# The expert stage of a two-layer diffusion transformer: steps of four bundles in another order, tiled products, and the scatter in fp32r

## The chip, the cores and the metric

One core of a Trainium2 chip runs the whole program: TensorE (PE; its weight loads are shown as PEld), VectorE (DVE), ScalarE (ACT), GpSimd (POOL) and SyncE (SP), which issues most DMAs. The metric is the device time of one execution in microseconds (us).

## What is computed

Two layers on 256 tokens of 1024 features (and 256 context tokens). Layer 0 has a mixer and a dense feed-forward part; layer 1 has a mixer and then a mixture of experts, which the change is about:

```python
def moe_swiglu(t, wr, br, w1, w3, w2):
    tf = t.reshape(-1, shape[-1])
    logits = (tf @ wr + br).astype(jnp.float32)
    top_v, top_i = lax.top_k(logits, TOP_K)              # TOP_K = 2 of N_EXPERTS = 8
    gates = jax.nn.softmax(top_v, axis=-1)
    dense_gate = jnp.sum(jax.nn.one_hot(top_i, N_EXPERTS) * gates[..., None], axis=1)
    for e in range(N_EXPERTS):                           # w1, w3: 1024 x 2816, w2: 2816 x 1024
        out = out + dense_gate[:, e:e + 1] * swiglu(tf, w1[e], w3[e], w2[e])
```

All is fp32. The result is multiplied by a gate vector of the layer (G2 in the kernel) and added to the residual X.

## The kernel before

**Routing and dispatch.** route() finds each token's two experts, orders experts 1 to 7 by how many tokens they got, and gives each token a slot in its expert. The experts' numbers become registers on SP (values_load, L1359), since SP needs them for the addresses of the weights; expert 0 of the order is always expert 0 and needs none. dispatch() makes, for a "quad" of four groups of 32 slots, a 0/1 matrix P, gathers the tokens by products with P (L1400), transposes them (L1411) into X, and makes P's transpose PT and the gates gs of the slots (L1420 to L1431).

**Bundles.** BUNDLES has four: bundle 0 is expert 0 with one group of 32 ("alone"); bundle 1 has two quads on experts 1 and 2 (the first quad is all expert 1, called quad A here; the second, quad B, has experts 1, 2, 2, 2); bundle 2 has one quad on experts 5 and 6; bundle 3 two quads on experts 3, 4 and 7.

**Steps.** The 2816 hidden features are cut into chunks of 1024, 1024 and 768 (CHUNKS). A step t is one chunk of one bundle: up(t, 0) multiplies by w1 and applies silu, up(t, 1) multiplies by w3 and multiplies both, turn(t) transposes the result (L1547), down(t) multiplies by w2 and adds into the accumulators yacc (L1585, L1587). moe_phases gives the order: up(t, 0), down(t - 1), up(t, 1), then the next t. Before the change steps 0 to 2 are bundle 0, 3 to 5 bundle 1, and so on. Each up and down runs in quarters of 256 rows of weights. After a bundle's last chunk, finish() multiplies yacc by gs and G2 (L1603) and scatters it with fp32 products by PT (L1608), each added to X (L1610). Dispatch, turn and finish are generators: pump(), called after each quad and row block of an up or down, advances them, so that their products stand between the experts' own.

**Products.** In the alone bundle four 256-column products go to four 32-column tiles of the array (L1493, L1574). For the other quads products() issues one 128 x 128 product of up to 512 columns if all four groups have one expert (L1498: quad A), else four products in 32-column tiles (L1502). A product of fp32 operands is two records in the trace.

**Weights.** plan_moe lists every weight load (1 MiB, or 0.75 MiB for up in the last chunk) in the order of use. ahead() issues loads on SP (L200) for as many entries as the ring has tiles: nine (three of the weights pool and EXTRA = 6), and, from the expert stage on, the four tiles that held split weights in earlier stages (whi and wlo), 13 in all. A tile is free again when the products that read it are done. moe() extends the ring by the four after route(). A pool's tag with bufs=n has n buffers, and a new tile waits for the one it replaces.

Of the kernel before, what the change touches and what calls it, by code (L numbers as in the profile page):

```python
# [48 lines left out]
CHUNKS = ((0, 1024), (1024, 1024), (2048, 768))  # L49

# [61 lines left out]
class Net:  # L112
    def __init__(self, tc, I, out):
        self.tc, self.nc, self.I, self.out = tc, tc.nc, I, out
        self.es = ExitStack()
        self.cnt = {}
        self.xw = None
        self.ring = deque()
        self.share = self.after = None
        self.tasks = []  # L120
        self.plan, self.pos = [], 0
# [63 lines left out]
    def plan_w(self, key, src, shape, split=True):  # L185
        parts = src if isinstance(src, list) else [(0, 128, src)]
        self.plan.append(dict(key=key, parts=parts, shape=shape, split=split, raw=None, hl=None))

    def ahead(self, raws=None, splits=None):
# [1125 lines left out]
    def route(self, p, t, first):  # L1315
# [29 lines left out]
        R = t.tile([128, 7, 7], F32, name="R")  # L1345
# [32 lines left out]
    def dispatch(self, p, quad, X, out):  # L1378
# [29 lines left out]
        for m in range(2):  # L1408
# [3 lines left out]
            dst = X[:, m * 4:m * 4 + 4].rearrange("p k t -> p (k t)")  # L1412
            if m:
                v.tensor_copy(dst, pg)
            else:
                nc.scalar.activation(dst, pg, AF.Copy)
# [6 lines left out]
        PT = p.tile([128, 2, 128], F32, tag="PT1h", name="PT1h", bufs=4)  # L1423
        gs = p.tile([128, 1], F32, tag="gs", name="gs", bufs=4)
# [18 lines left out]
    def moe_phases(bundles):  # L1443

        n = len(bundles) * len(CHUNKS)
# [8 lines left out]
    def plan_moe(self, tag, bundles):  # L1454
        for kind, t, m in self.moe_phases(bundles):
            bundle = bundles[t // len(CHUNKS)]
            c0, n = CHUNKS[t % len(CHUNKS)]
            rs = sorted({r for quad in bundle for r, _ in quad})
            for i in range(4 if kind == "up" else n // 256):
                for r in rs:  # L1460
                    if kind == "up":
                        src = self.moe_src(("moe_w1", "moe_w3")[m], r, slice(i * 256, (i + 1) * 256), slice(c0, c0 + n))
                        self.plan_w((tag, kind, t, m, i, r), src, (2, n), False)
                    else:
                        src = self.moe_src("moe_w2", r, slice(c0 + i * 256, c0 + (i + 1) * 256), slice(0, D))
                        self.plan_w((tag, kind, t, m, i, r), src, (2, D), False)

    def experts(self, p, tag, bundles, started=None):
# [6 lines left out]
        nch = len(CHUNKS)  # L1475
        ready = {0: started} if started is not None else {}
        acc, st = {}, {}

        def start(b):
            if b in ready or b >= len(bundles):  # L1480
                return
# [6 lines left out]
        def products(quad, outs, lhs, w, n, first, last):  # L1488

            if quad[0] == quad[1]:  # L1490
                for s in range(n // 256):
                    ss = slice(s * 32, s * 32 + 32)
                    mm(outs[0][ss, 0:256], lhs[:, ss], w[quad[0][0]][:, s * 256:(s + 1) * 256], start=first, stop=last, tile_position=(0, s * 32))  # L1493
                return
            for h in range(len(outs)):
                cs = slice(h * 512, min(n, h * 512 + 512))
# [3 lines left out]
                for s, (r, _) in enumerate(quad):  # L1500
                    ss = slice(s * 32, s * 32 + 32)
                    mm(outs[h][ss, 0:cs.stop - cs.start], lhs[:, ss], w[r][:, cs], start=first, stop=last, tile_position=(0, s * 32))  # L1502

        def parts(quad, n):
            return [256] if quad[0] == quad[1] else [min(512, n - c) for c in range(0, n, 512)]

        def places(quad, n):
            return n // 8 if quad[0] == quad[1] else 128

        def experts_of(bundle):  # L1510
            return sorted({r for quad in bundle for r, _ in quad})

        def up(t, m):
            b, (c0, n) = t // nch, CHUNKS[t % nch]
            bundle = bundles[b]
            ph = [[self.ps("ph") for _ in parts(quad, n)] for quad in bundle]
            for i in range(4):
                w = {r: self.W((tag, "up", t, m, i, r)) for r in experts_of(bundle)}
                for k in range(2):
                    kk = i * 2 + k  # L1520
                    for q, quad in enumerate(bundle):
                        products(quad, ph[q], ready[b][q][0][:, kk], {r: x[:, k] for r, x in w.items()}, n, kk == 0, kk == 7)
                        self.pump()
# [3 lines left out]
            for q, quad in enumerate(bundle):  # L1527
                for h, wd in enumerate(parts(quad, n)):
                    ps = slice(0, places(quad, n))
# [6 lines left out]
        def turn(t):  # L1536

            b, (c0, n) = t // nch, CHUNKS[t % nch]
            hid = []
            for q, quad in enumerate(bundles[b]):  # L1540
                g = p.tile([128, 8, 128], F32, tag="gt", name="gt", bufs=2)
                m = places(quad, n)
                for h, wd in enumerate(parts(quad, n)):
                    pt = self.ps("ptg")
                    nf = wd // 128
                    for f in range(nf):
                        nc.tensor.transpose(pt[:, f * m:(f + 1) * m], st[t][q][h][0:m, f * 128:(f + 1) * 128], self.ident[0:m, 0:m])  # L1547
                    dst = g[:, h * 4:h * 4 + nf, 0:m]
# [9 lines left out]
        def down(t):  # L1558
            b, (c0, n) = t // nch, CHUNKS[t % nch]
            bundle = bundles[b]  # L1560
            py = [[self.ps("py") for _ in parts(quad, D)] for quad in bundle]
            for i in range(n // 256):
                w = {r: self.W((tag, "down", t, 0, i, r)) for r in experts_of(bundle)}
                for f in range(2):
                    ff = i * 2 + f
                    for q, quad in enumerate(bundle):
                        g = st[t][q]
                        if quad[0] == quad[1]:

                            s = ff // 2  # L1570
                            lhs = g[:, ff % 2, s * 32:s * 32 + 32]
                            for s in range(4):
                                ss = slice(s * 32, s * 32 + 32)
                                mm(py[q][0][ss, 0:256], lhs, w[quad[0][0]][:, f, s * 256:(s + 1) * 256], start=ff == 0, stop=ff == n // 128 - 1, tile_position=(0, s * 32))  # L1574
                        else:
                            products(quad, py[q], g[:, ff], {r: x[:, f] for r, x in w.items()}, D, ff == 0, ff == n // 128 - 1)
                        self.pump()
                self.ahead()
            if c0 == 0:
                acc[b] = [p.tile([128, 2, 512], F32, tag="yacc", name="yacc", bufs=3) for _ in bundle]  # L1580
            for q, quad in enumerate(bundle):
                for h, wd in enumerate(parts(quad, D)):
                    y, o = acc[b][q][:, h, 0:wd], py[q][h][:, 0:wd]
                    if c0 == 0:
# [4 lines left out]
        def finish(b):  # L1589

            for q, quad in enumerate(bundles[b]):
                _, PT, gs = ready[b][q]
                y = acc[b][q]
                if quad[0] == quad[1]:
                    z = p.tile([128, 2, 512], F32, tag="yacc", name="yacc", bufs=3)
                    nc.gpsimd.memset(z, 0.0)
                    for s in range(4):
                        ss, cs = slice(s * 32, s * 32 + 32), slice(s * 256, s * 256 + 256)
                        v.scalar_tensor_tensor(z[ss, s // 2, s % 2 * 256:s % 2 * 256 + 256], y[ss, 0, 0:256], gs[ss], self.G2[ss, cs], op0=ALU.mult, op1=ALU.mult)
                    y = z  # L1600
                else:
                    for m in range(2):
                        v.scalar_tensor_tensor(y[:, m], y[:, m], gs, self.G2[:, m * 512:(m + 1) * 512], op0=ALU.mult, op1=ALU.mult)  # L1603
                yield 2
                for m in range(2):
                    for b2 in range(2):
                        po = self.ps("po")
                        mm(po, PT[:, b2], y[:, m], start=True, stop=True)  # L1608
                        x = self.X[:, b2, m * 512:(m + 1) * 512]
                        v.tensor_tensor(x, x, po, op=ALU.add)  # L1610
                        yield 1

        start(0)
        for kind, t, m in self.moe_phases(bundles):
            b, c = divmod(t, nch)
            if kind == "up":
                if c == 0 and m == 0:
                    self.until(lambda: len(ready[b]) == len(bundles[b]))
                if c == 1 and m == 0:
                    start(b + 1)  # L1620
# [3 lines left out]
            else:  # L1624
                self.until(lambda: not isinstance(st[t][0], list))
                down(t)
                if c == nch - 1:
# [3 lines left out]
    def moe(self, gp):  # L1631
        nc = self.nc
        with self.pool("moeb") as p:
# [13 lines left out]
            def first():  # L1647
                X = self.pa.tile([128, 8, 128], F32, tag="xq", name="xt", bufs=1)
# [100 lines left out]
```

## Time and profile before

| | us |
|---|---|
| median of 3 runs (1588.46 to 1591.87) | 1588.87 |
| the profiled execution | 1592.42 |
| its span, first to last instruction | 1590.6 |
| TensorE busy in it | 1504.1 |
| the expert stage in it, first to last expert product | 847.1 to 1576.4 |

Busy time of TensorE is a union of modelled intervals; in the expert stage it counts products that wait for nothing and products stretched by a lower clock alike. The granted clock (PEclk) is a share of 2.4 GHz; its lower level is 1.2 GHz. The profile's page lists DMA rates by slices; the expert weights are 264 MiB in all.

### The profile page before, as it was taken

Reading aid. Unit: us, or ns where it says so; the run is one execution under the profiler, and the core shown is the slowest. Engines: PE = TensorE matmul, PEld = TensorE weight load, DVE = VectorE, ACT = ScalarE, POOL = GpSimd, SP = SyncE. Lnnn points to the kernel's source line nnn. Section 1 sums busy time; section 2 is a strip of 40 time slices with the busy share of each in tenths; the row PEclk is TensorE's granted clock in tenths of the full one; section 3 lists DMA queues with packets and bytes.
Section 4 is the critical chain, followed back from the end, with each engine's and each line's share of the span. In section 5 each row is a group of like instructions: output and inputs, shape, how many; then the busy total and the mean of one; then the engine's idle time right before and its main releaser. Section 6 shows DMA issues by size and latency. Waiting matters only on the chain.

```text
span 1590.6 us, 22491 instructions
## 1 busy us (share of the span) xinstructions
PE 1504.1 (95%) x9376; PEld 871.8 (55%) x9376; DVE 681.3 (43%) x1128; ACT 352.4 (22%) x566; POOL 146.2 (9%) x151
## 2 busy tenths in 40 slices
PE   5999899999999999979988699999999999999998
PEld 3766566888888887766765233223333333334443
DVE  3647856867788874778844002000113000200103
ACT  3325543322222222437622000000000000000000
POOL 1331212000000014151330000000000000000000
PEclk9999999999999999999888799999999999999999
DMA  9332462444566761231285998767898999999995
GB/s 343 137 133 96 156 221 70 142 162 150 177 219 211 253 197 55 64 111 54 70 291 218 415 416 350 280 221 271 313 376 341 414 415 417 416 417 416 415 413 219
DMA packets 151502, 399.77 MB, mean 251 GB/s; under 512 B 10153, under 2 KB 38185, under 8 KB 151393
## 3 DMA queue, kind: packets, MB, share of 16 engines
q1 hardware_dynamic: 150688, 396.69, 66.6%
q8 instruction: 75, 1.23, 0.3%
q0 software_dynamic: 416, 1.05, 0.3%
q10 hardware_dynamic: 288, 0.52, 0.1%
q14 instruction: 35, 0.28, 0.0%
HBM read 397.14 MB, written 1.10 MB: 250 GB/s over the span
## 4 chain that ended last, share of the span: by engine, by line
PE 74%; DVE 9%; DMA 7%; POOL 4%; ACT 3%; issue 1%; SPq 0%; ACTq 0%; DVEq 0%; POOLq 0%
PE ph L1502 19%; PE py L1502 9%; DMA raw<-in_moe_w_dram 6%; PE ph L1498 5%; PE ph L227 5%; PE ph L226 5%; PE ph L225 5%; PE py L1498 3%; PE py L227 2%; PE ps L225 2%; PE py L226 2%; PE ps L227 2%; PE ps L226 2%; PE py L225 2%; PE po L1608 1%
## 5 line engine op out<-in xcount | busy, mean ns | idle before, releaser
L1502 PE MATMUL ph<-raw,xt 128*32 128x512 f32 (+1 forms) x3072 | 339.2, 560 | 1.7 <-DMA raw<-in_moe_w_dram 1.7
L1502 PEld LDWEIGHTS ph<-raw,xt 128*32 128x32 f32 x3072 | 111.5, 109 | 203.8 <-issue 184.6
L1502 PE MATMUL py<-raw,gt 128*32 128x512 f32 x1408 | 169.1, 595 | 3.1 <-DMA raw<-in_moe_w_dram 3.1
L207 ACT ACTIVATE whi<-raw 128x2048 fp32r<-128x2048 f32 x58 | 111.1, 1915 | 195.7 <-issue 61.4
L209 DVE TENSOR_TENSOR wlo<-raw,whi 128x2048 fp32r<-128x2048 f32 (+1 forms) x58 | 132.6, 2286 | 47.7 <-ACT whi L207 47.3
L1534 DVE TENSOR_TENSOR silu<-silu,ph 128x512 f32<-128x512 f32 (+2 forms) x33 | 20.2, 623 | 307.6 <-PE ph L1502 164.1
L227 PE MATMUL ph<-hTh,wlo 128*128 128x512 f32 (+1 forms) x384 | 145.5, 379 | 0.8 <-DVE wlo L209 0.8
L226 PE MATMUL ph<-hTl,whi 128*128 128x512 f32 (+1 forms) x384 | 144.6, 377 | 0.0
L225 PE MATMUL ph<-hTh,whi 128*128 128x512 f32 (+1 forms) x384 | 144.2, 376 | 0.0
L1587 DVE TENSOR_TENSOR yacc<-yacc,py 128x512 f32<-128x512 f32 (+1 forms) x22 | 14.5, 662 | 255.2 <-PE py L1502 129.3
L1502 PEld LDWEIGHTS py<-raw,gt 128*32 128x32 f32 x1408 | 52.3, 109 | 110.1 <-issue 98.1
L225 PE MATMUL ps<-whi,hTh 128*128 128x512 f32 (+1 forms) x272 | 108.4, 405 | 4.0 <-ACT hTh L159 2.1
L432 DVE SCALAR_TENSOR_TENSOR macc<-raw,cv,macc 128x512 f32<-128x512 f32 x154 | 111.1, 750 | 2.3 <-DMA raw<-in_w_mod_dram 1.2
L227 PE MATMUL ps<-whi,hTl 128*128 128x512 f32 (+1 forms) x272 | 105.9, 393 | 0.0
L226 PE MATMUL ps<-wlo,hTh 128*128 128x512 f32 (+1 forms) x272 | 105.3, 390 | 0.0
L1553 ACT ACTIVATE gt<-ptg 128x512 f32<-128x512 f32 (+2 forms) x18 | 10.1, 559 | 410.3 <-PE ptg L1547 269.5
L1498 PE MATMUL ph<-raw,xt 128*128 128x512 f32 x192 | 89.1, 587 | 1.6 <-DMA raw<-in_moe_w_dram 1.6
L226 PEld LDWEIGHTS ph<-hTl,whi 128*128 128x128 f32 x384 | 72.2, 188 | 15.3
L227 PEld LDWEIGHTS ph<-hTh,wlo 128*128 128x128 f32 x384 | 72.2, 188 | 15.0 <-DVE wlo L209 1.0
L225 PEld LDWEIGHTS ph<-hTh,whi 128*128 128x128 f32 x384 | 72.3, 188 | 14.5
L226 PE MATMUL py<-wlo,gh 128*128 128x512 f32 x176 | 69.1, 392 | 0.4 <-DVE wlo L209 0.4
L225 PE MATMUL py<-whi,gh 128*128 128x512 f32 x176 | 67.8, 391 | 0.0
(343 smaller groups left out, 1916.8 us busy)
## 6 DMA issues: line engine op xcount, KB each, us to landing
raw<-in_moe_w_dram SPq DMA_DIRECT2D x216, 1024.0 KB, 17.6
raw<-in_w_mod_dram SPq DMA_DIRECT2D x48, 1024.0 KB, 5.2
raw<-in_moe_w_dram SPq DMA_DIRECT2D x64, 768.0 KB, 15.3
raw<-in_ffn_w_dram SPq DMA_DIRECT2D x33, 1024.0 KB, 5.4
raw<-in_e_w_in_dram SPq DMA_DIRECT2D x10, 1024.0 KB, 7.1
raw<-in_w_out_dram SPq DMA_DIRECT2D x8, 1024.0 KB, 6.3
raw<-in_o_w_in_dram SPq DMA_DIRECT2D x7, 1024.0 KB, 5.4
ga<-dram SPq DMA_DIRECT2D x6, 512.0 KB, 4.9
```

The source lines that it names most:

```text
L207: nc.scalar.activation(hi, raw, AF.Copy)
L209: nc.vector.tensor_tensor(lo[:, :, n:], raw[:, :, n:], hi[:, :, n:], op=ALU.subtract)
L225: mm(o, lh, rh, start=start, stop=False)
L226: mm(o, lh, rl, start=False, stop=False)
L227: mm(o, ll, rh, start=False, stop=stop)
L432: v.scalar_tensor_tensor(a, raw[:, k], c, a, op0=ALU.mult, op1=ALU.add)
L1498: mm(outs[h][:, 0:cs.stop - cs.start], lhs, w[quad[0][0]][:, cs], start=first, stop=last)
L1502: mm(outs[h][ss, 0:cs.stop - cs.start], lhs[:, ss], w[r][:, cs], start=first, stop=last, tile_position=(0, s * 32))
L1534: v.tensor_tensor(s, s, o, op=ALU.mult)
L1553: nc.scalar.activation(dst, src, AF.Copy)
L1587: v.tensor_tensor(y, y, o, op=ALU.add)
L1608: mm(po, PT[:, b2], y[:, m], start=True, stop=True)
```

## The change

- The twelve steps run in the order ORDER: two chunks of bundle 0, then the first of bundles 1 and 2, the last of 0, then chunks of 1 and 2 in turn, and bundle 3 at the end. A bundle's dispatch is started at the first up of the step before its first.
- A quad of a bundle with more than one expert always uses four 32-column tiles; quad A is the one that this alters. The last chunk's 768 columns are cut 384 + 384 instead of 512 + 256.
- finish() takes both quads of a bundle together, half of the columns at a time: gating (DVE), a split into two fp32r parts (ACT rounds, DVE subtracts), then per 128 tokens one accumulation of two fp32r products for each quad and one add to X. For the alone bundle it scatters with 32-row tiles and needs no padded copy.
- The last step's down does not add into the accumulators. finish() scatters the first two chunks beside that down; the last quarter of the down does column half 0 first, then half 1; end() then gates out of PSUM and scatters in fp32.
- The ring is extended, and loads are issued, at the top of moe(), ahead of route(); entries of experts 1 to 7 are marked late and are not issued until the expert registers exist. The first dispatch writes a tile with 32 columns a block instead of 128. Bundle 1's accumulators lie in the rows of X that held the routed input; buffers of PT and gs go from 4 to 6.

```diff
@@ constants
+ORDER = (0, 0, 1, 2, 0, 1, 2, 1, 2, 3, 3, 3)
@@ Net.plan_w / ahead
-    def plan_w(self, key, src, shape, split=True):
+    def plan_w(self, key, src, shape, split=True, late=False):
...
         for w in self.plan[self.pos:end]:
+            if w["late"] and self.eidx is None:
+                break
@@ dispatch
-            dst = X[:, m * 4:m * 4 + 4].rearrange("p k t -> p (k t)")
+            dst = X[:, m * 4:m * 4 + 4]
+            src = pg.rearrange("p (k t) -> p k t", k=4)[:, :, 0:dst.shape[2]]
...
-        PT = p.tile([128, 2, 128], F32, tag="PT1h", name="PT1h", bufs=4)
-        gs = p.tile([128, 1], F32, tag="gs", name="gs", bufs=4)
+        PT = p.tile([128, 2, 128], F32R, tag="PT1h", name="PT1h", bufs=6)
+        gs = p.tile([128, 1], F32, tag="gs", name="gs", bufs=6)
@@ moe_steps, plan_moe
+    def moe_steps(order):
+        return [(b, order[:i].count(b)) for i, b in enumerate(order)]
...
+                        self.plan_w((tag, kind, t, m, i, r), src, (2, n), False, r > 0)
@@ experts
-        def products(quad, outs, lhs, w, n, first, last):
...
-                if quad[0][0] == quad[3][0]:
-                    mm(outs[h][:, 0:cs.stop - cs.start], lhs, w[quad[0][0]][:, cs], start=first, stop=last)
-                    continue
...
+        def parts(quad, n):
+            if is_alone(quad):
+                return [slice(0, 256)]
+            m = min(n // 2, 512)
+            return [slice(c, c + m) for c in range(0, n, m)]
...
+        def product(bundle, quad, out, lhs, w, cs, first, last):
+            n = cs.stop - cs.start
+            if len(self.experts_of(bundle)) == 1:
+                mm(out[:, 0:n], lhs, w[quad[0][0]][:, cs], start=first, stop=last)
                 return
+            for s, (r, _) in enumerate(quad):
+                ss = slice(s * 32, s * 32 + 32)
+                mm(out[ss, 0:n], lhs[:, ss], w[r][:, cs], start=first, stop=last, tile_position=(0, s * 32))
...
+        def gated(b, q, y, cs, ps=slice(0, 128)):
+            gs = ready[b][q][2]
+            return v.scalar_tensor_tensor(y[0], y[1], gs[ps], self.G2[ps, cs], op0=ALU.mult, op1=ALU.mult)
+        def scatter(b, ys, h):
+            for b2 in range(2):
+                po = self.ps("po")
+                for q, y in enumerate(ys):
+                    PT = ready[b][q][1][:, b2]
+                    for i, x in enumerate(y):
+                        one = PT if x.dtype == F32R else PT.bitcast(F32)
+                        mm(po, one, x, start=q + i == 0, stop=q + 1 == len(ys) and i + 1 == len(y))
+                x = self.X[:, b2, h * 512:(h + 1) * 512]
+                v.tensor_tensor(x, x, po, op=ALU.add)
+                yield 1
+        def finish(b):
...
+                    for s in range(4):
+                        ss = slice(s * 32, s * 32 + 32)
+                        gated(b, q, (y[ss], y[ss]), slice(s * 256, s * 256 + 256), ss)
+                    yield 2
...
+                            mm(po, PT[ss, b2].bitcast(F32), y[ss], start=True, stop=True, tile_position=(s * 32, 0))
+                            v.tensor_tensor(self.X[:, b2, cs], self.X[:, b2, cs], po, op=ALU.add)
...
+            for h in range(2):
+                cs = slice(h * 512, h * 512 + 512)
+                ys = []
+                for q in range(len(bundle)):
+                    y = acc[b][q][:, cs]
+                    gated(b, q, (y, y), cs)
+                    hi, lo = self.row("yh", F32R), self.row("yl", F32R)
+                    self.split(hi, lo, y)
+                    ys.append((hi, lo))
+                yield 2
+                yield from scatter(b, ys, h)
+        def down(t, final):
...
+                for hs in ((0,), (1,)) if i == ni - 1 else ((0, 1),):
...
+            if final:
+                return py
+            if c == 0:
+                acc[b] = [p.tile([128, 256], F32, tag="yq", name="yacc", bufs=1) if is_alone(quad) else
+                          self.X[:, 2 + q] if b == 1 else p.tile([128, D], F32, tag="yacc", name="yacc", bufs=2)
+                          for q, quad in enumerate(bundle)]
...
+        def end(b, py):
+            for h in range(2):
...
+                    y = p.tile([128, 512], F32, tag="silu", name="yend", bufs=4)
+                    gated(b, q, (y, py[q][h]), cs)
+                    ys.append((y,))
+                yield from scatter(b, ys, h)
...
+                if m == 0:
+                    if c == 0:
+                        self.until(lambda: len(ready[b]) == len(bundles[b]))
+                    begin(t + 1)
...
+                if t == n - 1:
+                    self.spawn(finish(b))
+                py = down(t, t == n - 1)
+                if t == n - 1:
+                    self.drain()
+                    for _ in end(b, py):
+                        pass
+                elif c == len(CHUNKS) - 1 and t < n - 1:
                     self.spawn(finish(b))
@@ moe
+        self.ring.extendleft([(self.wp, kind, 2) for kind in ("whi", "wlo") for _ in range(2)])
+        self.ahead()
         with self.pool("moeb") as p:
...
-                X = self.pa.tile([128, 8, 128], F32, tag="xq", name="xt", bufs=1)
+                X = self.pa.tile([128, 8, 32], F32, tag="xa", name="xa")
...
-            self.ring.extendleft([(self.wp, kind, 2) for kind in ("whi", "wlo") for _ in range(2)])
-            with self.tc.issue_after(last.ins):
-                self.ahead()
-            self.experts(p, 0, BUNDLES, zero)
+            self.ahead()
+            self.experts(p, 0, BUNDLES, ORDER, zero)
```

## Rows read from the trace of the kernel before

**Rows 1.** The page: share of the chain by engine, and the expert weights' loads.
```profile
PE 74%; DVE 9%; DMA 7%; POOL 4%; ACT 3%; issue 1%; SPq 0%; ACTq 0%; DVEq 0%; POOLq 0%
...
raw<-in_moe_w_dram SPq DMA_DIRECT2D x216, 1024.0 KB, 17.6
...
raw<-in_moe_w_dram SPq DMA_DIRECT2D x64, 768.0 KB, 15.3
```
**Rows 2.** Three stretches: length, busy us (instructions) by engine, clock, DMA share, GB/s.
```profile
847.10:909.57 62.47, 46.15 (x534) 23.26 (x533) 10.24 (x42) 5.76 (x11) 0.00 (x0) 0.86 0.92 363
909.57:1190.37 280.80, 280.80 (x1656) 92.26 (x1660) 24.70 (x46) 15.22 (x27) 0.00 (x0) 0.99 0.84 322
1190.37:1576.38 386.01, 381.22 (x3368) 145.95 (x3359) 42.11 (x72) 20.06 (x35) 0.00 (x0) 1.00 0.99 398
```
**Rows 3.** Single windows of 10 us, same columns.
```profile
870.00:880.00 10.00, 4.18 (x68) 1.59 (x63) 0.00 (x0) 0.39 (x1) 0.00 (x0) 0.97 1.03 418
880.00:890.00 10.00, 7.73 (x60) 2.98 (x55) 0.42 (x1) 0.38 (x1) 0.00 (x0) 0.52 1.03 411
910.00:920.00 10.00, 10.00 (x45) 3.31 (x44) 0.00 (x0) 0.33 (x1) 0.00 (x0) 0.83 1.02 414
1030.00:1040.00 10.00, 10.00 (x58) 2.94 (x51) 0.00 (x0) 0.00 (x0) 0.00 (x0) 1.00 0.77 284
1340.00:1350.00 10.00, 8.85 (x64) 2.54 (x64) 0.00 (x0) 0.53 (x1) 0.00 (x0) 1.00 1.03 419
```
**Rows 4.** Chain in order of time: start us, us, what.
```profile
877.76 31.67 DMA raw<-in_moe_w_dram x2
909.57 3.26 PE ph L1498 x4
...
926.49 1.91 PE ph L1498 x4
928.40 1.85 PE ph L1502 x16
...
1266.97 17.84 DMA raw<-in_moe_w_dram
1576.38 7.28 PE po L1608 x16
```
**Rows 5.** Timeline in bundle 0: start us, us, engine, line, operation.
```profile
849.11 6.67 PE L1493 MATMUL ph<-raw,xt 128*32 128x256 f32 x116
913.25 0.33 ACT L1553 ACTIVATE gt<-ptg 128x192 f32<-128x192 f32 x1 [22.15 <-PE ptg L1547]
```
**Rows 6.** Chain around bundle 3's dispatch.
```profile
1202.54 1.06 PE po L1608 x2
1213.28 3.67 PE pg L1400 x16
1220.30 1.75 PE pgt L1411 x16
1224.96 0.22 PE ptd L1420 x2
1225.17 0.35 PE ptd L1422 x4
```
**Rows 7.** SP: its issues ahead of the expert stage, and its wait for the registers.
```profile
831.67 0.37 SPq L200 DMA_DIRECT2D raw<-in_moe_w_dram  x1
852.22 11.59 SPq L200 DMA_DIRECT2D raw<-in_moe_w_dram  x9
SPq L1359 <- DVE over L1361: 16.3, 1, 16.3
```
**Rows 8.** Groups by shape: mean ns of one.
```profile
L1603 DVE SCALAR_TENSOR_TENSOR yacc<-yacc,gs,ga 128x512 f32<-128x512 f32 x10 | 7.3, 748 | 0.1
L1416 ACT ACTIVATE xt<-pgt 128x512 f32<-128x512 f32 x6 | 3.6, 598 | 10.1 <-PE pgt L1411 10.1
```
**Rows 9.** The last add to X.
```profile
1583.68 0.69 DVE L1610 TENSOR_TENSOR X<-X,po 128x512 f32<-128x512 f32 x1 [0.17 <-PE po L1608]
```

More of the change, by code (lines that the diff above doesn't have):

```diff
@@ L1513, in up, with product_alone @@
+        def product_alone(out, lhs, w, n, first, last):
+            for s in range(n // 256):
+                mm(out[s * 32:s * 32 + 32, 0:256], lhs, w[:, s * 256:(s + 1) * 256], start=first, stop=last, tile_position=(0, s * 32))
         def up(t, m):
-            b, (c0, n) = t // nch, CHUNKS[t % nch]
+            b, c = steps[t]
+            n = CHUNKS[c][1]
             bundle = bundles[b]
@@ L1517, in up @@
             for i in range(4):
[L1518 removed]
+                w = {r: self.W((tag, "up", t, m, i, r)) for r in self.experts_of(bundle)}
                 for k in range(2):
                     kk = i * 2 + k
+                    wk = {r: x[:, k] for r, x in w.items()}
                     for q, quad in enumerate(bundle):
[L1522 removed]
+                        lhs = ready[b][q][0][:, kk]
+                        if is_alone(quad):
+                            product_alone(ph[q][0], lhs, wk[quad[0][0]], n, kk == 0, kk == 7)
+                        else:
+                            for h, cs in enumerate(parts(quad, n)):
+                                product(bundle, quad, ph[q][h], lhs, wk, cs, kk == 0, kk == 7)
                         self.pump()
@@ L1527, in up @@
             for q, quad in enumerate(bundle):
-                for h, wd in enumerate(parts(quad, n)):
-                    ps = slice(0, places(quad, n))
+                for h, cs in enumerate(parts(quad, n)):
+                    ps, wd = slice(0, places(quad, n)), cs.stop - cs.start
                     s, o = st[t][q][h][ps, 0:wd], ph[q][h][ps, 0:wd]
@@ L1560, in down @@
+        def down(t, final):
+            b, c = steps[t]
+            n = CHUNKS[c][1]
             bundle = bundles[b]
             py = [[self.ps("py") for _ in parts(quad, D)] for quad in bundle]
[L1562 to L1577, printed above, removed]
-                self.ahead()
@@ L1579, in down @@
-            if c0 == 0:
-                acc[b] = [p.tile([128, 2, 512], F32, tag="yacc", name="yacc", bufs=3) for _ in bundle]
+            ni = n // 256
+            for i in range(ni):
+                w = {r: self.W((tag, "down", t, 0, i, r)) for r in self.experts_of(bundle)}
+                for hs in ((0,), (1,)) if i == ni - 1 else ((0, 1),):
+                    for f in range(2):
+                        ff = i * 2 + f
+                        a, z = ff == 0, ff == n // 128 - 1
+                        wf = {r: x[:, f] for r, x in w.items()}
+                        for q, quad in enumerate(bundle):
+                            g = st[t][q]
+                            if is_alone(quad):
+                                if 0 in hs:
+                                    s = ff // 2 * 32
+                                    product_alone(py[q][0], g[:, ff % 2, s:s + 32], wf[quad[0][0]], D, a, z)
+                            else:
+                                for h in hs:
+                                    product(bundle, quad, py[q][h], g[:, ff], wf, parts(quad, D)[h], a, z)
+                            self.pump()
+                self.ahead()
@@ L1587, in down @@
                         v.tensor_tensor(y, y, o, op=ALU.add)
[L1589 to L1611, printed above, removed]
@@ L1613, in experts, with begin @@
-        start(0)
-        for kind, t, m in self.moe_phases(bundles):
-            b, c = divmod(t, nch)
+        def end(b, py):
+            for h in range(2):
+                cs = slice(h * 512, h * 512 + 512)
+                ys = []
+                for q in range(len(py)):
+                    y = p.tile([128, 512], F32, tag="silu", name="yend", bufs=4)
+                    gated(b, q, (y, py[q][h]), cs)
+                    ys.append((y,))
+                yield from scatter(b, ys, h)
+        def begin(i):
+            if i < len(steps) and steps[i][1] == 0 and steps[i][0] not in ready:
+                start(steps[i][0])
@@ L1616, in experts @@
+        begin(0)
+        n = len(steps)
+        for kind, t, m in self.moe_phases(n):
+            b, c = steps[t]
             if kind == "up":
[L1617 to L1620, printed above, removed]
+                if m == 0:
+                    if c == 0:
+                        self.until(lambda: len(ready[b]) == len(bundles[b]))
+                    begin(t + 1)
```

90 lines of the change are left out of this document (43 added, 47 removed).

## The prediction

> **What bounds the kernel now.** I read the page's chain first, then the expert stage cut into stretches and windows, then its chain in order of time, then single instructions. The page puts 74% of the chain on TensorE and 7% on DMA [rows 1]; as an average that says little. Cut into three stretches, the expert stage (847.1 us, the first expert product, to 1576.38, the last) is three kernels [rows 2]; the single windows of 10 us inside them are [rows 3]. From 847.1 to 909.57 the DMA moves 363 GB/s and TensorE is busy 46 of 62 us, at a mean clock of 0.86; in windows DMA runs at 411 and 418 GB/s, TensorE is busy 4.18 and 7.73 of 10 us, and the clock falls to 0.52, so part of that time TensorE ran at 1.2 GHz. This is bundle 0, one expert with 32 tokens: many bytes, few products. From 909.57 to 1190.37, bundle 1, TensorE has no gap and DMA has room (322 GB/s; a single window 284). From 1190.37 to the end DMA is nearly full (398 GB/s; a window 419) while TensorE shows short gaps (8.85 of 10 us). So DMA and TensorE take turns as the bound, and each rests while the other works. The chain names the places [rows 4]: loads up to 909.4, and one of 17.84 us at 1266.97.
>
> **Prices.** The steady load rate is about 415 GB/s [rows 3], so 1 MiB takes 2.527 us; 216 loads of 1 MiB and 64 of 0.75 are 264 MiB [rows 1]. A 512-column group of four 32-column products is half of an "x16" piece: 1.85 / 2 = 0.925 us; the same columns as full 128x128 products (two products) take 1.91 / 2 = 0.955 [rows 4]. A 256-column product of bundle 0 is two records: 116 records in 6.67 us, 0.115 us a product [rows 5]. A scatter product between expert products costs 1.06 us, a transpose 1.75 / 16 = 0.11, an fp32r product 3.67 / 16 = 0.23 [rows 6].
>
> **Mixed order.** First stretch: before, it holds 62.5 us. Work in it: 176 up and 64 down products of bundle 0, 240 x 0.115 = 27.6; the dispatch of two quads, 3.67 + 1.75 + 2 x (0.22 + 0.35) = 6.6 as for bundle 3 [rows 6]; turns about 0.5. So 27.8 us are waiting. After the change only two steps of bundle 0 come first, then bundle 1. Loads: before, SP issues two of the four loads into the freed split buffers, the second at 831.67, then stands 16.3 us at the register load of L1359, and the other two go out behind it at 852.22 [rows 7]. That is 9 + 2 = 11 loads ahead; with the ring extended at the top of moe() all 13 are ahead of that wait. SP cannot stand longer for them than to 831.67, when it had already issued its last load. The first load behind the wait lands data from about 855.1 (32 MiB are needed at 909.57 minus about 1: 21 x 2.527 = 53.1 us before it). After: MiB number N lands at 855.1 + (N - 13) x 2.527. TensorE: two ups of 32 products (3.7 each) to 854.5, the third with the dispatch and a turn to 865.8, the down to 869.5. The last quarter of that down needs MiB 16 at 868.6, there at 862.7; the fourth up's last quarter MiB 20 at 872.3, there at 872.8; the last quarter of bundle 1's first up MiB 28 at about 897, there at 893.0. I take 2 of waiting for the stretch. **Gain 25.8**. The clock at bundle 1's start (0.83, its first full products 3.26 instead of 1.91) comes back too: **1.4** [rows 3, 4].
>
> Last stretch: 386.0 us. Work: 116 groups left of bundle 2 and 264 of bundle 3, 380 x 0.925 = 351.5; 12 scatter products x 1.06 = 12.7; one dispatch of two quads 6.6; 66 transposes of turns x 0.11 = 7.3; sum 378.1. So only 7.9 us are waiting, though the chain names loads such as that of 17.84 us there: most of each lies beside products. After, do the loads stay hidden? Between the start of bundle 1's first up (874) and the end of bundle 0's last up (1024) 58 MiB are used, 146.6 us of loading, against 144 groups (133.2), 80 small products (9.2) and some 7 of dispatch and turns, 149; from there to the start of bundle 3, 81 MiB, 204.7, against 240 groups (222) and some 21 of the rest, 243; bundle 3 with bundle 2's last down, 105 MiB, 265, against 276 groups (255.3) and some 11, 266. With up to 13 MiB ahead (33 us) this just holds; the thin place is around 1024, margin near zero. **Gain 7.9**, and between 874 and 1024 a few us could come back as waits.
>
> What would undo this part is a lower load rate: 251 MiB (264 - 13) from 855.1 to 1576 allow 2.87 us a MiB, 365 GB/s; below it no order helps. Full windows here moved 411 to 419 GB/s [rows 3]. The Trainium skill, in "DMA: Bandwidth & Descriptors" (Specifications), lists about 358 GB/s as HBM's limit for one core; by that figure the loads alone would end near 1590 and the time would stay as it is, an estimate from that page. This case's windows do not agree with it, and the sum goes by them.
>
> **All of bundle 1 in 32-column tiles.** Quad A has 132 such groups (two up chunks and a down of 16 each for 1024, 24 + 12 for 768): 132 x 0.03 = **4.0** gain, on the path since bundle 1 is TensorE's. Its neighbour quad B, three of whose tiles read one expert, runs at the price used. The order of full and tiled products also costs at each switch: a scatter product takes 1.06 between tiled ones [rows 6] against 7.28 / 8 = 0.91 in a row [rows 4], some 0.15.
>
> **Scatter.** Outside the tail, before: 16 products at 1.06 = 17.0. After, fp32r: bundle 1 four outputs x (4 x 0.23 + 0.15) = 4.3, bundle 2 four x (0.46 + 0.15) = 2.4, bundle 3's first two chunks 4.3, now inside the last down, and bundle 0 eight products of 32 rows x 256 columns. No row has that form: below, 0.115 as tiled products; above, 0.43, half of a full one without overlap. I take 0.3, the middle: 2.4. Sum 13.4, **gain 3.6** (ends 2.6 to 5.1). What it adds on the way: per half and quad, gating 0.75, ACT rounding 0.60, DVE remainder 0.69, as the add of the same shape [rows 8, 9]; ACT and DVE take turns on one quad, so two quads 4.1 us. "yield 2" gives TensorE two pumps of cover: in bundle 2's last chunk 2 x 2 x 0.694 = 2.8 us, so 1.3 of waiting twice, and DVE first has up to 0.7 of yacc adds; in bundle 3's down 3.7, so about 0.4 twice. **Loss 4.2** (ends 0, if the scheduler finds other products, to 7).
>
> **Small edits.** The first dispatch evicts 4 x 32 columns instead of 512 in front of the first product: 0.60 now on ACT, 0.33 for 192 columns [rows 5, 8]: **gain 0.4**. New short steps: turn of bundle 2's first chunk has to fit in bundle 0's last up (24 products, 2.8 us): multiply 0.69, transposes 0.88, copies 0.60 and 0.69: covered to within 0.5; other boundaries with four accumulators and four scatter outputs live may wait for a 0.69 add. **Loss 2** (0 to 8). The 384/384 cut streams the same columns as 512/256. The accumulator in X's rows, PT as fp32r and the moved tiles add no instruction. Dispatch of bundles 1 to 3 moves, unchanged in number, behind TensorE's own products.
>
> **Tail.** Before: last expert product 1576.4, eight fp32 scatter products 7.3, X adds to 1584.37, the store, end 1590.6 [rows 4, 9]. After: gating from PSUM of half 0 runs beside half 1's products, half 1's (1.5 us) beside half 0's scatter; then the same eight fp32 products on TensorE, one 0.69 add and the same store. The four yacc adds and the other four X adds weren't last. **0** (-1 to +2).
>
> **Sum.** 25.8 + 1.4 + 7.9 + 4.0 + 3.6 - 4.2 + 0.4 - 2 = 36.9. The profiled execution took 1592.42 us, its span 1590.6; so 1555.5 there. It lies 3.55 above the median of 1588.87, so the median should be 1588.87 - 36.9 = 1552.0.
>
> **Rivals.** (1) Loads stay the bound in places: margins near zero around 1024, one late slot after another. For: 398 GB/s over the last 386 us now; the balance in bundle 3 is 265 to 266. Against: 1489 is the earliest end of loading (855.1 + 251 x 2.527), 40 us ahead of TensorE. If the middle and last gains go half and the short steps cost their upper end, it gives 1552 + 4 + 6 + 4 = 1566. A load rate under 365 GB/s would leave 1589; the windows leave that 1 in 100. (2) The early loads do not get ahead of the register wait (SP order set otherwise by the scheduler): 2 x 2.527 = 5 us back, 1557. (3) The losses vanish: no split or boundary waits, tail shorter by 1: 1552 - 7 = 1545, and with the upper gains 1542. (4) Slower: quad A's four tiles now all read one expert's rows, and if those reads get in each other's way, the group costs more than 0.925. It decides from 36.9 / 132 = 0.28 us more a group (1.2); fully in series it would be 4 x 0.86 = 3.4 a group, 327 us, so about 1880. Against: quad B's tiles 1 to 3 read one expert and run at 1.85 a piece; I see nothing for it.
>
> **How the numbers follow.** Forecast 0.67, rival 2 0.05; rival 1 0.13; rival 3 0.11; rival 4 0.03; no change (load rate) 0.01. The range, 8 in 10, from 1542 (rival 3's end) to 1566 (rival 1). A measurement of this kernel tells about 0.2%, 3.2 us, from no change. Faster 0.96, same 0.01, slower 0.03.
>
> **What would show it.** Right: 13 expert loads issued before the register wait; the first product of bundle 1 near 874; clock 1.00 from 860 on; TensorE without gaps; the last expert product near 1539; DMA below 415 GB/s in most windows. Wrong: loads in the chain after 875; tiled pieces of bundle 1 above 1.85; TensorE waiting for the remainder of the split; a tail over 15 us.

## The result and the profile after

The changed kernel took 1536.15 us in the median of four runs (1533.84 to 1538.73), the kernel before, run beside it on the same chip, 1590.37 us: a ratio of 0.966 with a 95% interval of 0.9639 to 0.9681, or 54.2 us less. The forecast was 36.9 less, with a range that began at 1542. One run of the kernel with fewer products, below, took 1670.61 us at a mean clock of 0.741 where its others had 0.95, and it is left out of that kernel's median. The profiled execution after took 1535.58 us, its span 1533.7. Three lines of the page after: the span, the load rate in 40 slices, and the chain by engine.

```profile
span 1533.7 us, 24219 instructions
...
GB/s 356 142 138 83 166 200 116 87 211 115 165 211 222 219 269 95 56 98 83 55 141 272 336 416 417 416 416 416 416 413 408 362 370 417 416 417 414 406 415 59
...
PE 78%; DVE 9%; POOL 4%; ACT 4%; DMA 3%; issue 1%; SPq 0%; ACTq 0%; DVEq 0%; POOLq 0%
```

DMA fell from 7% to 3% of the chain [rows 1]. The expert stage now runs from 844.53 to 1520.25 us, 675.7 us against 729.3 before [rows 2], so 53.6 of the 56.9 us between the two spans lie in it. It starts 2.6 us earlier, and that is not the change's: the two profiled executions are already 3.8 us apart at the same split of weights, ahead of any changed code. A point of time in one trace can therefore be compared with the same point in another only to a few us. Before:

```profile
745.86 2.20 DVE wlo L209
```

After:

```profile
742.09 2.20 DVE wlo L214
```

The stretches of the expert stage after; columns as in [rows 2].

```profile
844.53:874.46 29.93, 26.53 (x371) 16.68 (x371) 8.90 (x39) 4.77 (x9) 0.00 (x0) 1.00 0.82 325
874.46:1180.00 305.54, 303.28 (x2902) 107.40 (x2906) 25.62 (x50) 18.60 (x33) 0.00 (x0) 0.99 1.03 415
1180.00:1240.00 60.00, 60.00 (x625) 26.54 (x618) 14.56 (x30) 5.62 (x10) 0.00 (x0) 1.00 0.92 350
1240.00:1488.36 248.36, 248.36 (x2303) 102.08 (x2303) 28.86 (x45) 15.69 (x27) 0.00 (x0) 1.00 1.02 414
1488.36:1520.25 31.89, 31.89 (x221) 10.90 (x221) 7.88 (x12) 2.13 (x4) 0.00 (x0) 1.00 0.32 129
```

Where before one engine rested while the other worked (363 GB/s with TensorE idle a quarter of the time, then 322 GB/s with TensorE full), both are now full at once: TensorE loses 5.7 us of 676, and from 874 to 1488 loads run at 414 or 415 GB/s but for one lull between 1180 and 1240. The chain after in order of time: start us, us, what.

```profile
856.19 18.14 DMA raw<-in_moe_w_dram
874.46 3.54 PE ph L1521 x16
...
911.62 29.18 PE ph L1521 x272
...
955.73 27.47 PE py L1521 x256
...
1006.07 15.50 DMA raw<-in_moe_w_dram
...
1216.70 20.60 PE py L1521 x192
...
1489.82 3.56 PE py L1521 x24
1493.38 1.13 PE po L1593 x4
...
1499.21 3.56 PE py L1521 x28
1502.77 0.67 PE po L1593 x2
1503.44 1.85 PE py L1521 x12
...
1510.65 9.60 PE py L1521 x79
1520.25 7.08 PE po L1593 x16
1527.35 0.69 DVE X L1595
```

L1521 is the tiled product, L1593 the scatter; in kernels below with full products these are L1517. 955.73 and 911.62 are the lines on which the forecast broke. 256 records are 32 tiled groups of 512 columns: 27.47 / 32 = 0.858 us a group, and 29.18 / 34 = 0.858. The forecast's price was 0.925, half of 1.85 [rows 4].

### The profile page after: what moved, and what is told of

It is laid out like the page before. It is cut to its first block, busy times and chain, and to the rows that moved or that the text cites. A ratio compares the mean times of both kernels' runs of the same rounds, so it can differ in the third digit from the quotient of the medians.

```text
span 1533.7 us, 24219 instructions
## 1 busy us (share of the span) xinstructions
PE 1462.2 (95%) x10240; PEld 872.1 (57%) x10240; DVE 686.9 (45%) x1138; ACT 357.8 (23%) x576; POOL 145.2 (9%) x150
## 4 chain that ended last, share of the span: by engine, by line
PE 78%; DVE 9%; POOL 4%; ACT 4%; DMA 3%; issue 1%; SPq 0%; ACTq 0%; DVEq 0%; POOLq 0%
PE ph L1521 26%; PE py L1521 12%; PE ph L232 5%; PE ph L231 5%; PE ph L230 5%; PE ps L230 3%; PE py L232 2%; PE py L231 2%; PE ps L232 2%; PE ps L231 2%; PE py L230 2%; DMA raw<-in_moe_w_dram 2%; DVE wlo L214 1%; PE po L1593 1%; POOL hrs L237 1%
## 5 line engine op out<-in xcount | busy, mean ns | idle before, releaser
L1521 PE MATMUL ph<-raw,xt 128*32 128x512 f32 (+1 forms) x3840 | 402.7, 561 | 4.2 <-DMA raw<-in_moe_w_dram 4.2
L1521 PEld LDWEIGHTS ph<-raw,xt 128*32 128x32 f32 x3840 | 143.8, 110 | 233.8 <-issue 217.0
L1521 PE MATMUL py<-raw,gt 128*32 128x512 f32 x1760 | 198.6, 593 | 0.0
L1555 DVE TENSOR_TENSOR silu<-silu,ph 128x512 f32<-128x512 f32 (+3 forms) x33 | 20.6, 623 | 262.4 <-PE ph L1521 228.9
L1521 PEld LDWEIGHTS py<-raw,gt 128*32 128x32 f32 x1760 | 68.4, 110 | 122.0 <-issue 119.4
L1665 DVE TENSOR_TENSOR yacc<-yacc,py 128x512 f32<-128x512 f32 (+1 forms) x10 | 6.3, 634 | 160.6 <-PE py L1521 103.2
L1575 ACT ACTIVATE gt<-ptg 128x512 f32<-128x512 f32 (+3 forms) x18 | 9.5, 530 | 294.0 <-PE ptg L1569 294.0
L232 PE MATMUL py<-whi,gl 128*128 128x512 f32 x176 | 66.8, 394 | 0.0
```

Of the source, the lines that this page charges most:

```text
L232: mm(o, ll, rh, start=False, stop=stop)
L1521: mm(out[ss, 0:n], lhs[:, ss], w[r][:, cs], start=first, stop=last, tile_position=(0, s * 32))
L1555: v.tensor_tensor(s, s, o, op=ALU.mult)
L1575: nc.scalar.activation(dst, src, AF.Copy)
L1665: v.tensor_tensor(y, y, o, op=ALU.add)
```

## The experiments

The kernel before ran at 1589.9 to 1591.11 us beside these kernels. "After" is the changed kernel, 1536.15 us; line numbers differ by a few between kernels.

**What quad A's tiles are worth.** The first kernel is the one before with only this part of the change:

```diff
-                if quad[0][0] == quad[3][0]:
+                if len(w) == 1:
```

> The kernel before with one edit: quad A of bundle 1 in four 32-column tiles, nothing else. Theory S (a switch between full and tiled products costs TensorE, and the 0.925 us a group of my prediction held one such switch for every two groups): tiled groups of bundle 1 fall to 0.86 us, an x16 piece from 1.85 to 1.72; the stretch of bundle 1 (280.8 us) shortens by 132 x (0.955 + 0.925 - 2 x 0.86) = 21 us; loads are the bound later, so of that some 15 to 21 reach the end: 1570 to 1576 beside 1590. Rival P (the price of my prediction: 0.03 us a group): 4 us, 1586.

Measured: 1568.36 us (1565.99 to 1570.61), ratio 0.986 [0.9844, 0.9877], 21.8 us less than before; a little below even the switch theory's band. Rival P's 4 us falls. Its chain in bundle 1, with L1502 as the tiled product:

```profile
1005.58 27.47 PE py L1502 x256
```

The second is the kernel after with that part undone:

```diff
-            if len(self.experts_of(bundle)) == 1:
+            if quad[0][0] == quad[3][0]:
```

> The kernel after with quad A put back to full 128 x 128 products. Theory S: 21 us of TensorE time come back in bundle 1's steps; loads now have more slack there, so of the 21 some 10 to 18 show: 1546 to 1554 beside 1536. Rival P: 4 us, 1540. If loads alone bounded the kernel after: 1536.

Measured: 1555.85 us (1554.07 to 1556.12), ratio 0.9782 [0.9766, 0.9799], 19.7 more than after. Quad A's part is about 20 us from either side, not 4.0. Both theories gave too little here. The chain alternates:

```profile
889.70 1.91 PE ph L1517 x4
891.61 1.85 PE ph L1521 x16
```

These two runs do not say whether the full product itself is dearer or the change between full and tiled. The third kernel keeps the second's full products and halves the number of changes: in bundle 1, all rows of a load go to one quad before the next.

```diff
+        def turns(b):
+            nq = len(bundles[b])
+            if b == 1:
+                return [(k, q) for q in range(nq) for k in range(2)]
+            return [(k, q) for k in range(2) for q in range(nq)]
...
-                for k in range(2):
...
-                    for q, quad in enumerate(bundle):
+                for k, q in turns(b):
...
-                    for f in range(2):
...
-                        for q, quad in enumerate(bundle):
+                    for f, q in turns(b):
```

> The changed kernel with quad A in full products, as in the run before with that edit (1555.85 us), but bundle 1 takes both rows of a load for one quad before the next quad, so that four full products and then four tiled groups stand in a row and only half as many changes between full and tiled products are left; the products themselves are the same in number and shape. Theory switch (each change between full and tiled products costs about 0.135 us, and a full product by itself hardly more than a tiled group): 66 changes fewer, some 9 us, so 1546 to 1549, and the pieces of the chain read about 3.6 us for x8 full and 3.55 for x32 tiled. Rival (the full product itself is the dearer one, 0.955 us against 0.858, and the change costs nothing): the time stays at 1554 to 1557.

Measured: 1543.78 us (1542.82 to 1545.46), ratio 0.97 [0.9683, 0.9717]: 12.1 less than with the changes in place, past the switch theory's 1546. The rival falls. Chain of this kernel:

```profile
891.14 3.63 PE ph L1517 x8
894.77 3.57 PE ph L1521 x32
```

Two more full products add 3.63 - 1.91 = 1.72 us, two more tiled groups 3.57 - 1.85 = 1.72: 0.86 a group in either form, the same as in a long run. What is left is the change: 1.91 - 1.72 = 0.19 into full, 1.85 - 1.72 = 0.13 into tiled products as the chain divides them, 0.32 for both. Bundle 1 had 66 such pairs, 66 x 0.32 = 21; this kernel has 33 fewer, 10.6, and 12.1 was measured. Going to and fro between quads costs nothing by itself: the kernel after does so too, at 0.858 a group. The Trainium skill, in "TensorEngine Tiling (Array Packing)" (Tiling Modes), says that changing the tiling mode, not just the tile, drains TensorE. This case's traces agree, and put the price of a change at 0.13 to 0.19 us.

**The order.** The kernel after, with the steps of one bundle after another:

```diff
-ORDER = (0, 0, 1, 2, 0, 1, 2, 1, 2, 3, 3, 3)
+ORDER = (0, 0, 0, 1, 1, 1, 2, 2, 2, 3, 3, 3)
```

> The kernel after with the steps of the kernel before, one bundle after the other; tiles, scatter, early loads and tail stay. Theory S with loads as the bound in bundles 0, 2 and 3: the waiting at bundle 0 (27.8 less 5 of the early loads) and some of the last stretch come back: +25 to +35, 1561 to 1571. Rival (the order is worth little once the tiles are cheap, because loads bound everything): +5 to +10, 1541 to 1546.

Measured: 1562.06 us (1561.11 to 1562.81), ratio 0.9824 [0.9807, 0.984], 25.9 more than after, as the theory said. Windows of this kernel (columns as above) and the loads in its chain:

```profile
870.00:910.00 40.00, 32.76 (x309) 17.69 (x313) 6.85 (x22) 3.48 (x7) 0.00 (x0) 0.87 1.03 413
910.00:1180.00 270.00, 270.00 (x2597) 95.79 (x2589) 34.49 (x64) 17.30 (x30) 0.00 (x0) 1.00 0.91 352
1180.00:1545.00 365.00, 361.84 (x3208) 139.42 (x3210) 40.20 (x68) 23.61 (x41) 0.00 (x0) 1.00 0.99 400
```

```profile
858.49 17.64 DMA raw<-in_moe_w_dram
...
1295.27 17.77 DMA raw<-in_moe_w_dram
```

The shape of before is back: waits at the start, room on the DMA (352 GB/s) while TensorE is full, waits again late.

**The early loads.** The kernel after, with the ring extended behind the register wait again:

```diff
-        self.ring.extendleft([(self.wp, kind, 2) for kind in ("whi", "wlo") for _ in range(2)])
-        self.ahead()
...
-            self.ahead()
+            self.ring.extendleft([(self.wp, kind, 2) for kind in ("whi", "wlo") for _ in range(2)])
+            with self.tc.issue_after(last.ins):
+                self.ahead()
```

> The kernel after with the ring extended behind route() as before, so that two of the four loads again go out behind the register wait. If loads bound the first two thirds of the stage: 2 x 2.5 = 5 us, 1541. If TensorE bounds: 0 to 1, 1536 to 1537.

Measured: 1543.48 us (1541.76 to 1543.75), ratio 0.9705 [0.9689, 0.9721]: 7.3 more, where 5 was expected if loads are the bound.

```profile
746.61 2.20 DVE wlo L214
...
865.94 18.00 DMA raw<-in_moe_w_dram
...
884.07 3.64 PE ph L1521 x16
...
1528.27 7.08 PE po L1593 x16
```

The traces put it lower. This profiled execution is 4.5 us later than after's already at the split of weights (746.61 against 742.09), ahead of the edit. Bundle 1's first product comes 9.6 us later (884.07, not 874.46), so 5.1 are the edit's, the two loads of the expectation; at the end of the last expert product (1528.27 against 1520.25) 3.5 of it are left. So the early loads are worth 3.5 to 7.3 us.

**The split scatter.** The kernel after, with one fp32 product in place of the two fp32r:

```diff
-                    hi, lo = self.row("yh", F32R), self.row("yl", F32R)
-                    self.split(hi, lo, y)
-                    ys.append((hi, lo))
+                    ys.append((y,))
```

> The kernel after with finish() scattering the gated accumulator in one fp32 product for each quad, without the split into two fp32r parts. TensorE does 20 products of 0.86 instead of 40 of 0.23: +8 us of its time. If the split makes TensorE wait as forecast (4.2 us), those go: net +4, 1540. If the split is hidden: +8 where TensorE is the bound, less where loads are; the part inside the last down (3 us) lies behind the last load and shows in any case: 1539 to 1544. If loads hide all but that: 1539.

Measured: 1540.8 us (1540.4 to 1542.39), ratio 0.9696 [0.9679, 0.9714], 4.7 more than after. That is close to the 1540 expected if the split makes TensorE wait and inside the 1539 to 1544 expected if it does not, so the time alone does not tell the two apart. An output of two quads takes 1.91 us in this kernel, and 1.13 after:

```profile
1240.04 1.91 PE po L1593 x4
```

**The last chunk.** The kernel after, with the last down collected in yacc and the whole scatter of bundle 3 behind it:

```diff
-                if t == n - 1:
-                    self.spawn(finish(b))
-                py = down(t, t == n - 1)
-                if t == n - 1:
-                    self.drain()
-                    for _ in end(b, py):
-                        pass
-                elif c == len(CHUNKS) - 1 and t < n - 1:
+                down(t, False)
+                if c == len(CHUNKS) - 1:
```

> The kernel after with the last chunk of bundle 3 added into the accumulators and one finish() after it, all in fp32r; nothing is scattered beside the last down. By the forecast (tail worth 0, scatter inside the down 4.3 + 0.8): the down 5 us shorter, the tail 4 to 5 us longer (add 0.7, split 1.3, a second half behind the first), about 1536. Theory T (beside that, the products of the last down stand in a worse order when scatter products are put among them: 25.7 us for 24 groups that take 20.6 in a row): the down 10 us shorter, 1530 to 1532.

Measured: 1528.66 us (1527.92 to 1529.84), ratio 0.962 [0.9603, 0.9637]: 7.5 less than after, past theory T's 1530, and the fastest of these kernels that does the whole work. Chain of its end:

```profile
1491.02 21.66 PE py L1521 x192
...
1512.70 0.69 DVE yacc L1665
...
1519.83 0.50 DVE X L1595
```

The last down is one piece of 21.66 us; after, from 1489.82 to 1520.25, it is 30.43, 8.8 more. Its five scatter pieces make 4.7 of that. The rest is in the products, which take 25.7 after (3.56 + 3.56 + 3.56 + 1.85 + 3.56 + 9.60): the scatter cuts them into pieces whose four tiles are not filled alike. The piece of 12 records takes 1.85 us, as 16 records do; those of 24 and 28 take 3.56, as 32 do (3.57). By the starts in the trace the 12 come three at a time. Of the 24 of the first piece, 16 have begun by 1491.40, four at a time, and the other 8 come two at a time:

```profile
1489.75 1.94 PE L1521 MATMUL py<-raw,gt 128*32 128x512 f32 x16
```

From the last expert product to the end of the span it is 1526.2 - 1512.68 = 13.5 us here and 13.4 after: the early scatter gave no shorter tail. But the edit also lets the tail here scatter in fp32r, where after's is in fp32; what an early scatter with the same tail would save was not tried. The last down begins 1.2 us later here; 8.8 - 1.2 is the 7.5. How much of the 1.2 belongs to the edit is open, since executions differ by that much ahead of changed code.

**How far the loads are.** The kernel after, without the second and third load's products in the ups of bundles 1 to 3 (half of those up products; every load stays):

```diff
+                        if i in (1, 2) and not is_alone(quad):
+                            self.pump()
+                            continue
```

> The kernel after without the products of the second and third quarter of every up of bundles 1 to 3 (half of the up products are left out; all loads stay). It measures the floor that loads set: 251 MiB x 2.527 = 634 us from about 852, the last load at 1486, then the last quarter of a down (8 to 10 us) and the tail (13.4): span 1508 to 1512, time 1510 to 1514. If loads do not run through even without competition for tiles: more. TensorE's work falls by 189 us, so were it the only bound, 1350.

Measured: 1519.61 us (1519.54 to 1521.89), ratio 0.956 [0.954, 0.9581]. With half of the up products gone, TensorE's busy time falls by 17% in the first and by 25% in the last of the windows below, at a lower clock, and the whole by only 16.5 us: the loads hold it there. Windows of this kernel:

```profile
860.00:1180.00 320.00, 259.78 (x2237) 99.35 (x2238) 30.61 (x69) 20.56 (x37) 0.00 (x0) 0.93 1.03 416
1180.00:1240.00 60.00, 59.92 (x522) 26.37 (x516) 20.13 (x39) 7.26 (x13) 0.00 (x0) 0.97 1.03 415
1240.00:1480.00 240.00, 181.15 (x1398) 70.71 (x1395) 25.04 (x38) 15.04 (x26) 0.00 (x0) 0.88 1.03 417
```

The first and the last of them in the kernel after:

```profile
860.00:1180.00 320.00, 314.51 (x3090) 114.00 (x3087) 29.52 (x67) 19.49 (x36) 0.00 (x0) 0.99 1.03 415
1240.00:1480.00 240.00, 240.00 (x2208) 97.26 (x2211) 27.20 (x42) 15.69 (x27) 0.00 (x0) 1.00 1.03 414
```

After's lull is gone here. It is worth 60 x (1 - 350 / 415) = 9.4 us of loading, most of the 13.6 between the two spans (1533.7 and 1520.1). My figure of 1510 to 1514 was too low.

**An order without the lull?** The kernel after, with bundle 0's last step moved back:

```diff
-ORDER = (0, 0, 1, 2, 0, 1, 2, 1, 2, 3, 3, 3)
+ORDER = (0, 0, 1, 2, 1, 2, 2, 1, 0, 3, 3, 3)
```

> The kernel after with another order: 0, 0, 1, 2, 1, 2, 2, 1, 0, 3, 3, 3, bundle 0's last chunk after those of 1 and 2. Theory S with loads as bound until about 1190 and TensorE from there to 1240: the wait for loads around 1006 to 1021 (10 us of waiting) goes, and the loads that ran short at 1200 to 1240 (303 to 361 GB/s) are fed by bundle 0's: 8 to 11 us less, 1525 to 1528. If the order no longer matters: 1536.

Measured: 1535.64 us (1533.27 to 1536.13), ratio 0.9658 [0.9641, 0.9675]: no difference from after. The theory of 8 to 11 us more gain missed.

```profile
860.00:1060.00 200.00, 196.80 (x1902) 71.31 (x1903) 15.02 (x40) 14.90 (x26) 0.00 (x0) 0.99 1.02 416
1060.00:1160.00 100.00, 99.58 (x960) 37.28 (x955) 10.33 (x15) 3.97 (x7) 0.00 (x0) 1.00 0.99 391
1160.00:1240.00 80.00, 79.54 (x835) 34.36 (x831) 16.40 (x33) 7.48 (x14) 0.00 (x0) 1.00 1.03 413
1240.00:1480.00 240.00, 240.00 (x2267) 96.11 (x2262) 30.84 (x52) 15.64 (x27) 0.00 (x0) 1.00 1.02 413
```

The lull moved to 1060 to 1160 and TensorE stayed as busy: 615.92 us of the 620 in these rows, where after it was 614.51. The lull is no loss by itself: TensorE is full during it, and SP waits for a tile to come free. Between 1180 and 1240 in the trace after it waited 31.2 + 17.2 us for expert products to end.

## Why the prediction was too small

The sign and the mechanism of the order held. One price did not, and it carries most of the miss; three smaller terms were off as well.

**The step that failed: "All of bundle 1 in 32-column tiles", 4.0 us.** I took 0.925 us for a tiled group and 0.955 for a full one from pieces of the chain that alternate [rows 4], so both prices held a change of mode, and the difference of the two, 0.03, told nothing of what happens when the alternation ends. With the price of a run, 132 groups x (0.955 + 0.925 - 2 x 0.858) = 21.6; measured 21.8 alone and 19.7 on top of the rest. Of the 17.3 us by which the whole gain was larger than forecast, this term makes 15.7 to 17.8. I had seen the switch, "some 0.15" for a scatter product, and put it on the scatter only. The price of a run stood in the trace before, in bundle 3, as 31 groups at 0.858 each. So did a piece of 24 records between scatter products that takes as long as 32 records:

```profile
1358.35 3.56 PE ph L1502 x24
...
1421.68 26.61 PE py L1502 x248
```

**The same price in the last stretch.** "Only 7.9 us are waiting" was 386.0 less 378.1 of work at 0.925 a group. At 0.858 the 380 groups take 326, the rest 26.6 as before, and 33 us remain. In only 4.8 of them is TensorE without a product (381.22 busy of 386.01 [rows 2]). The other 28.6 lie inside its busy time: changes of mode, pieces with unevenly filled tiles, and products that stand beside a wait for another expert's load; how they divide was not tried. The loads take the time too: the bytes of that stretch, 386.0 us at 398 GB/s [rows 2], need 370 at 415, so without bytes moved ahead of it only 16 of the 33 were to be had. This is worked out, not tried by itself.

**Order and early loads, 25.8 + 1.4 + 7.9 = 35.1.** Measured 25.9 for the order and 7.3 for the early loads, 33.2 together in medians. Rival 2 put the early loads at 5, and 3.5 to 7.3 is what the run and its trace give. Two steps behind it held: the 13 loads went out ahead of the register wait, at which SP then stood 15.1 us, and the thin place came near 1024 (a load of 15.50 in the chain at 1006.07). From the first expert product to bundle 1's first it took 29.9 us, where the forecast has 26.9 (847.1 to 874); 3.4 of it are without a product, where 2 were taken. The 1.4 for the clock did not come: TensorE was busy 1.23 of the 4.46 us before bundle 1's first products, these ran at a granted clock of 0.52, near the lower level, and took 3.54 us instead of 1.85.

```profile
870.00:874.46 4.46, 1.23 (x20) 0.45 (x17) 0.42 (x1) 0.00 (x0) 0.00 (x0) 1.00 1.01 405
874.46:878.00 3.54, 3.54 (x17) 0.77 (x18) 0.00 (x0) 0.00 (x0) 0.00 (x0) 0.52 1.03 422
```

**Two signs of being right failed.** "DMA below 415 GB/s in most windows" was wrong: it runs at 414 or 415 but for the lull. "TensorE without gaps" missed by 5.7 us, and a load stands in the chain after 875, which was named as a sign of being wrong. Both engines are full. With the right price of a group I would have named the loads as the next bound: with half of the up products left out the time falls by only 16.5 us.

**Scatter and split, 3.6 - 4.2 = -0.6.** The 3.6 held, the 4.2 did not. Outside the tail the scatter products take 13.0 us after: in bundle 1 four of 1.13, in bundle 2 2.46 in all, in the last down 4.7, in bundle 0 two pieces of 0.64, 1.3 where 2.4 was forecast. Before they took 17.0, so 4.0 are gained. The feared waits are small: the largest of TensorE for an operand of the scatter that I found in the trace after is 0.8 us.

```profile
1057.39 0.64 PE po L1611 x8
```

The 4.7 measured is another quantity: the edit takes back the split alone and keeps both quads in one accumulation. By the products it should be 7.8: 0.78 for each of eight outputs of two quads (1.91 to 1.13) and 0.39 for each of four of one quad (1.06 to 0.67). Of that 4.7 arrived; where the other 3 went was not tried apart.

**Tail, 0.** The tail is 13.4 us against 14.2, as forecast. But the scatter that moved into the last down costs its own 4.7 us there, which the forecast had at 4.3, and leaves the tiles of the down unevenly filled, which it had at nothing: with one finish() behind the down instead, the time is 7.5 us less.

**The sum.** 33.2 + 19.7 + 4.7 - 7.5 = 50.1 of 54.2, with the split standing for the whole scatter. The first dispatch and the short steps (0.4 - 2) were not tried alone; the 4 us that are left may be theirs, or come from undoing parts one at a time where two bounds lie close together, or from the differences between executions of a few us. That stays open. Rival 4 fell: four tiles that read one expert's rows run at 0.858 a group. Rival 1, loads as the bound in places, came true in the windows and yet the time was shorter than the forecast.

## What to carry to other kernels

Price an operation in the neighbourhood that it will have after the change: a piece that alternates with another form holds the change of form, and the price of a run has to be looked up where such a run stands in the trace (here in bundle 3 of the kernel before). If a faster engine leaves two bounds a few us apart, ask of each further term which of the two it moves. Work that is moved beside a packed group of products may cost more there than behind it, if it cuts the products into pieces whose tiles are unevenly filled.

## What the runs showed of the hardware

Full and tiled fp32 products of the same columns cost the same in a row: 0.86 us for 512 columns, as four products in 32-column tiles or as one full product. A change costs 0.19 us into full and 0.13 into tiled products. A piece of tiled products takes as long as its fullest tile needs: 12 records, three at a time, take 1.85 us as 16 do, and 24 take 3.56, as 32 do (3.57). The loads held 415 and 414 GB/s over 306 and 248 us beside a TensorE that was busy 99% and all of the time.

The Trainium skill, in "DMA: Bandwidth & Descriptors" (Specifications), lists about 358 GB/s as HBM's limit for one core, a stack's bandwidth divided by its two cores. This program runs on one core, and its loads were above that figure; the measurement decides.
